# The fourth tile for U blocks ahead of the loop, kept in use for the last four blocks

## The chip, the cores and the metric

The kernel runs on one core of a Trainium2 chip. The metric is the time of one execution on the device in microseconds (us); the median of several executions counts. The engines are named as in the profile: PE (TensorE matmuls), DVE (VectorE), ACT (ScalarE), POOL (GpSimd) and SP (SyncE, which here only issues DMAs). ACT and POOL issue DMAs as well. Each engine takes its own instructions in their order; semaphores order them between engines.

## The reference

One encoder layer on 512 tokens of width 1024: LayerNorm, a joint projection, neighbourhood attention and latent attention, an output projection, LayerNorm, and then a feed-forward part with 16384 experts (PEER) and a gated embedding, followed by a last LayerNorm. The change sits in the feed-forward part, for a chunk of 128 tokens:

```
q = (xb @ w_q).reshape(128, 8, 256)
s1, s2 = q[..., :128] @ sub_keys[0].T, q[..., 128:] @ sub_keys[1].T
...top 16 of each, top 16 of their sums -> idx (128 tokens x 128 experts), g = softmax
u = u_table[idx]                       # 16384 x 1024
hpre = einsum('td,ted->te', xb, u)
act = g * gelu(hpre)
out = einsum('te,ted->td', act, v_table[idx])
```

## The kernel before

The 16384 experts are 128 blocks of 128. For most tokens the kernel does not gather rows: it multiplies every token with every expert and masks with a dense matrix G (tokens x experts, zero where an expert was not chosen).

**Which tokens go which way.** Chunk 0 (128 tokens) gathers its U and V rows by indirect DMAs of POOL, 128 of each (`gather_u`, L1349, and `gather_v`, L1358, into eight tiles `gat`; 26 of the U rows are done earlier, in `beside`, L1076); DVE multiplies each gathered tile. Chunk 1 gathers its U rows (`own_rows`). Chunks 2 and 3 (256 tokens) use dense U blocks: a block is 1024 x 128 numbers, 512 KB, and gives `ge = gelu(U block x tokens)`. For chunks 1 to 3 (384 tokens) V is dense.

**U blocks ahead of the loop.** Blocks 0 to 99 are computed before the main loop, by `lead_block` (L1134): eight float32 matmuls of 128x256 with `whole` (the 256 tokens), sixteen in the profile's records, 3.5 us a block. They fill PE while DVE routes and builds G. A block is loaded by `load_u` (L1102) through SP's DMA queue into one of four tiles: three tiles `raw` of the pool `wst`, taken in turn, and one tile `raw_u`, for every fourth block. A load waits until the last reader of its tile is done. Before the change the last four blocks (96 to 99) take `raw` tiles alone, so that `raw_u` has its last reader in block 95, and block 99 takes the tile of block 96. The matmuls of blocks 97 to 99 write PSUM tiles `hp`, those before them `mm`.

**What takes the place of raw_u.** After the blocks the pool of `raw_u` is closed (`pR.close()`, L1333), and tiles of the next pools are laid over it, among them one of the eight `gat` tiles: its first indirect DMA on POOL waits until the last matmul that reads `raw_u` is done.

**The main loop** (L1392) has 128 steps n. In each, DVE masks G (`dn`, L1426), ACT and DVE split the step's V block and its slice of G into two parts (`v_hi`, `v_lo`, `a_hi`, `a_lo`, L102 and L103), and PE adds 18 matmuls of 128x512 into `acc` (L1377). From n = 8 to n = 35 a step also has one of the U blocks 100 to 127 (`expert_in`, L789, 24 matmuls of 128x256, tiles `raw`, `whi`, `wlo`). Between these, DVE does gathers, one or two a step up to n = 8 and about three a step while U blocks last. V blocks come through SP (`v_raw`, three tiles, L1330), slices of G too (`gt`, four quarters, L1315); G was written to DRAM before, by twelve ACT-issued DMAs of 2 MB, four for each chunk (`g_dram<-g_st`, L1019, the last of them issued at 884.77 us).

**Order.** Up to the loop, all five queues keep the program's order (`manual_schedule`); in the loop only DVE and SP do. A load that is written earlier in the program stands earlier in SP's queue, and everything behind it waits with it. `h_s` and `gb` at L1086 are V blocks of the first two steps, loaded ahead.

Of the kernel before, what the change touches and what calls it, by code (L numbers as in the profile page):

```python
# [35 lines left out]
LEAD = 100  # L36
# [25 lines left out]
RAWS = 4  # L62
# [11 lines left out]
def tile_encoder_layer(ctx: ExitStack, tc: tile.TileContext, A: dict, out: bass.AP):  # L74
# [96 lines left out]
    def ps_tile(name, bufs=2):  # L171
        return ps6.tile([128, 512], F32, name=name, bufs=bufs)
# [924 lines left out]
    raws = []  # L1097
    tasks = []
    gating = True
    loaded = 0  # L1100

    def load_u():  # L1102
        nonlocal loaded
        if loaded < LEAD:
            if loaded % RAWS == RAWS - 1 and loaded < LEAD - 4:
                raw = rg.tile([128, 8, 128], F32, name="raw_u")
            else:
                raw = wst.tile([128, 8, 128], F32, name="raw", bufs=3)
            raws.append((loaded, raw))
            ins = nc.sync.dma_start(raw, A["uT"][loaded])  # L1110
            if not loaded:
                tc.keep_in_program_order(ins)
            loaded += 1
# [3 lines left out]
    def leave_u(i, ps):  # L1117
        k = i - SPILL
        if 0 <= k < KEPT:
            if k % 2 == 0:  # L1120
                name = ("g_raw", "g_raw", "g_hi", "g_lo")[k // 2]
                kept.append(pK.tile([128, 2, N_U], F32, name=name, bufs=2 if k < 4 else 1))
            ge = kept[k // 2][:, k % 2]
        else:
            ge = pB.tile([128, N_U], F32, name="ge", bufs=GES)
        nc.scalar.activation(ge, ps[:, :N_U], AF.Gelu)  # L1126
        if i < SPILL:
            nc.scalar.dma_start(ge_dram[i], ge)
        else:
            ge_t[i] = ge  # L1130
# [3 lines left out]
    def lead_block():  # L1134


        while len(raws) < (RAWS if loaded < LEAD - 4 else 3) and loaded < LEAD:
            load_u()
        if not raws:
            return  # L1140
        i, raw = raws.pop(0)
        ps = psH.tile([128, 512], F32, name="hp") if gating else ps_tile("mm", 4)
        for k in range(8):
            nc.tensor.matmul(ps[:, :N_U], raw[:, k], whole[:, k, :], start=(k == 0), stop=(k == 7))  # L1144
            if k == 3 and last:
                leave_u(*last.pop())
            if k % 2 and tasks:
                tasks.pop(0)()
            yield PRODUCT_U
        last.append((i, ps))  # L1150
# [52 lines left out]
    def gate_and_leads():  # L1203
        nonlocal gating
        graw = [gate_raw(0), gate_raw(1)]
        for n in range(FIRST):
            if n == FIRST - 2:
                w, cut = gate_cut(graw.pop(0))
                tasks.extend([cut[0], nothing, cut[1]])
            yield from lead_block()  # L1210
        for j in range(16):
            if j % 8 == 0:
                while tasks:
                    tasks.pop(0)()
                gps = [ps_tile("mm", 4) for _ in range(4)]
            k = j % 8
            for c in range(4):
                cs = slice(c * 128, (c + 1) * 128)
                mm3(gps[c], (hTh[:, k, cs], hTl[:, k, cs]), w, k == 0, k == 7)
                yield PRODUCT_G  # L1220
            if j + 1 < 16:
                w, cut = gate_cut(graw.pop(0))
                if j + 2 < 16:
                    graw.append(gate_raw(j + 2))
                tasks[0:0] = [cut[0], nothing, cut[1]]
            if k == 7:
                gate_end(gps, slice(j // 8 * 512, j // 8 * 512 + 512))
                yield from lead_block()
                yield from lead_block()
            yield from lead_block()  # L1230
# [34 lines left out]
    with tc.manual_schedule(engines={nc.vector.engine, nc.scalar.engine, nc.tensor.engine, nc.sync.engine,  # L1265
                                     nc.gpsimd.engine}):
        for _ in range(RAWS):
            load_u()
# [280 lines left out]
```

## Time and profile before

| | |
|---|---|
| median of 3 runs | 1527.5 us (1525.15 to 1528.54) |
| profiled execution, its own time | 1529.18 us |
| its span in the trace | 1527.2 us |
| PE busy | 1487.8 us (97%) |
| DVE busy | 1303.8 us (85%) |
| ACT, POOL busy | 658.2 us, 556.2 us |
| DMA, mean over the span | 301 GB/s |

Times in the rows are us from the start of the span. In a timeline row the columns are start, length, engine, line, operation, out<-in, shapes and count; in square brackets is the idle time of the engine before it, and what ended it. `SPq` is a DMA issue on SP's queue: its length is the issue, not the transfer. Blocks 0 to 99 lie between 410 and 910 us, the main loop from 909.5 us to 1510 us.

### The profile page before, as it was taken

The numbers are of one execution on the slowest core, as the hardware profiler recorded it, in microseconds if no ns is written. First come the engines' busy times: TensorE is split into PE (matmuls) and PEld (weight loads), VectorE is DVE, ScalarE is ACT, GpSimd is POOL, SyncE is SP. The second block draws the span as 40 slices with busy tenths as digits, with TensorE's granted clock in tenths as the row PEclk, the third lists the DMA queues.
The fourth block names the chain that finished last, engine by engine and source line by source line (L and its number), as shares of the span: only waits on it lengthen the run. The fifth ranks groups of instructions, "written<-read, shape, count | busy, mean of one in ns | idle before, by whom it ended". The sixth has DMA issues, their size and how long they took to land.

```text
span 1527.2 us, 23112 instructions
## 1 busy us (share of the span) xinstructions
PE 1487.8 (97%) x7747; PEld 1256.4 (82%) x7747; DVE 1303.8 (85%) x3020; ACT 658.2 (43%) x1226; POOL 556.2 (36%) x520
## 2 busy tenths in 40 slices
PE   8999899999999999999999989999999999999997
PEld 5788777788888889889888867888988888888885
DVE  6376686679989998888889947999999999999996
ACT  3355685333222666147515623343434333333342
POOL 1013110010015333353313424555555666666620
PEclk9999999999999999999999989999999999999999
DMA  6333240142379999999999988999999999999982
GB/s 229 102 111 97 84 125 29 42 142 83 104 228 334 346 408 383 413 398 415 406 379 353 410 353 304 415 411 414 415 411 411 410 412 410 410 412 411 412 321 77
DMA packets 194218, 459.38 MB, mean 301 GB/s; under 512 B 18226, under 2 KB 97970, under 8 KB 192564
## 3 DMA queue, kind: packets, MB, share of 16 engines
q1 hardware_dynamic: 121712, 214.08, 38.3%
q0 software_dynamic: 57984, 207.12, 34.6%
q10 hardware_dynamic: 14404, 36.71, 6.1%
q8 instruction: 61, 1.00, 0.3%
q14 instruction: 57, 0.47, 0.1%
HBM read 414.07 MB, written 40.89 MB: 298 GB/s over the span
## 4 chain that ended last, share of the span: by engine, by line
PE 79%; DVE 11%; DMA 6%; issue 2%; ACT 2%; POOL 0%; SPq 0%; DVEq 0%; ACTq 0%; POOLq 0%
PE acc L1377 33%; PE mm L1144 9%; PE hp L1144 4%; PE tr L1002 4%; PE mm L117 3%; PE mm L119 3%; PE mm L118 3%; PE pj L117 3%; PE pj L118 3%; PE pj L119 3%; DMA row<-in_u_rows_dram,s_ix 2%; PE hp L117 2%; PE hp L119 2%; PE hp L118 2%; DMA wlo<-in_u_rows_dram,s_ix 2%
## 5 line engine op out<-in xcount | busy, mean ns | idle before, releaser
L1360 POOL DMA_INDIRECT gat<-in_v_rows_dram,i_sel x128 | 211.4, 1652 | 120.2 <-DVE base L1362 99.2
L1144 PE MATMUL mm<-whole,raw 128*128 128x256 f32 x832 | 187.1, 379 | 0.9 <-DMA raw<-in_uT_dram 0.9
L102 ACT CAST whi<-raw 128x1024 fp32r<-128x1024 f32 (+4 forms) x117 | 117.3, 1003 | 149.8 <-PE mm L118 46.6
L1345 POOL DMA_INDIRECT gat<-in_u_rows_dram,i_sel x102 | 132.6, 1300 | 124.8 <-DVE hdot L1351 97.5
L1144 PEld LDWEIGHTS mm<-whole,raw 128*128 128x128 f32 x832 | 155.9, 190 | 21.2 <-ACT ge L1126 1.3
L1362 DVE SCALAR_TENSOR_TENSOR base<-gat,hdot,base 128x1024 f32<-128x1024 f32 x128 | 163.9, 1280 | 1.6
L103 DVE TENSOR_TENSOR wlo<-raw,whi 128x1024 fp32r<-128x1024 f32 (+4 forms) x117 | 135.5, 1159 | 33.2 <-ACT whi L102 32.9
L1377 PE MATMUL acc<-v_hi,a_hi 128*128 128x512 f32 x480 | 149.0, 391 | 2.4 <-ACT a_hi L102 2.2
L1377 PE MATMUL acc<-v_lo,a_hi 128*128 128x512 f32 x480 | 148.7, 390 | 0.1
L1377 PE MATMUL acc<-v_hi,a_lo 128*128 128x512 f32 x480 | 148.4, 389 | 0.0
L102 ACT CAST a_hi<-gt 128x384 fp32r<-128x384 f32 x126 | 64.6, 512 | 183.0 <-PE acc L1377 111.1
L102 ACT CAST v_hi<-v_raw 128x1024 fp32r<-128x1024 f32 x80 | 84.0, 1050 | 109.6 <-issue 58.1
L1057 POOL DMA_INDIRECT whi<-in_u_rows_dram,s_ix x51 | 53.8, 1055 | 200.6 <-DVE cand L905 132.3
L1351 DVE CUSTOM_DVE_ANT_0 scr<-gat,h 128x1024 f32<-128x1024 f32 x102 | 124.7, 1222 | 2.3
L1040 DVE TENSOR_SCALAR oh_j<-iota,eT 128x128 f32<-128x128 f32 x384 | 117.3, 379 | 0.0
L1377 PEld LDWEIGHTS acc<-v_lo,a_hi 128*128 128x128 f32 x480 | 90.0, 188 | 19.8 <-DVE v_lo L103 0.8
L1377 PEld LDWEIGHTS acc<-v_hi,a_lo 128*128 128x128 f32 x480 | 89.9, 188 | 19.1 <-DVE a_lo L103 0.2
L103 DVE TENSOR_TENSOR v_lo<-v_raw,v_hi 128x1024 fp32r<-128x1024 f32 x80 | 97.4, 1218 | 9.1 <-ACT v_hi L102 9.1
L1377 PEld LDWEIGHTS acc<-v_hi,a_hi 128*128 128x128 f32 x480 | 88.1, 188 | 19.9 <-ACT a_hi L102 3.0
L1002 PEld LDWEIGHTS tr<-oh_i,oh_j 128*128 128x128 f32 x768 | 94.3, 191 | 9.2 <-ACT g_st L1014 2.3
L1002 PE MATMUL tr<-oh_i,oh_j 128*128 128x128 f32 x768 | 97.2, 277 | 3.7 <-DVE oh_j L1040 3.7
L103 DVE TENSOR_TENSOR a_lo<-gt,a_hi 128x384 fp32r<-128x384 f32 x126 | 69.7, 553 | 33.2 <-ACT a_hi L102 31.8
(392 smaller groups left out, 3504.7 us busy)
## 6 DMA issues: line engine op xcount, KB each, us to landing
raw<-in_uT_dram SPq DMA_DIRECT2D x104, 512.0 KB
v_raw<-in_v_rows_dram SPq DMA_DIRECT2D x82, 512.0 KB
g_dram<-g_st ACTq DMA_DIRECT2D x12, 2048.0 KB
gt<-g_dram SPq DMA_DIRECT2D x60, 384.0 KB
raw<-in_v_rows_dram SPq DMA_DIRECT2D x44, 512.0 KB
raw_u<-in_uT_dram SPq DMA_DIRECT2D x24, 512.0 KB
ge_dram<-ge ACTq DMA_DIRECT2D x88, 128.0 KB
ge<-ge_dram SPq DMA_DIRECT2D x88, 128.0 KB
```

The lines of the kernel that those rows point to most:

```text
L102: nc.scalar.copy(hi, src)
L103: nc.vector.tensor_tensor(lo, src, r32(hi), op=OP.subtract)
L117: nc.tensor.matmul(ps, a[0], b[0], start=start, stop=False)
L118: nc.tensor.matmul(ps, a[0], b[1], start=False, stop=False)
L119: nc.tensor.matmul(ps, a[1], b[0], start=False, stop=stop)
L1002: nc.tensor.matmul(ps[:, i * 128:(i + 1) * 128], oj[:, 4 * r + i, :], oi[:, 4 * r + i, :], start=True, stop=True)
L1144: nc.tensor.matmul(ps[:, :N_U], raw[:, k], whole[:, k, :], start=(k == 0), stop=(k == 7))
L1345: nc.gpsimd.indirect_dma_start(out=u[:], out_offset=None, in_=u_rows, in_offset=bass.IndirectOffsetOnAxis(ap=i_sel[:, c, k:k + 1], axis=0))
L1351: nc.vector.tensor_tensor_reduce(scr, u, h[c], op0=OP.mult, op1=OP.add, accum_out=hdot[:, c, k:k + 1], scale=1.0, scalar=0.0)
L1360: nc.gpsimd.indirect_dma_start(out=u[:], out_offset=None, in_=v_rows, in_offset=bass.IndirectOffsetOnAxis(ap=i_sel[:, c, k:k + 1], axis=0))
L1362: nc.vector.scalar_tensor_tensor(base[c], u, hdot[:, c, k:k + 1], base[c], op0=OP.mult, op1=OP.add)
L1377: nc.tensor.matmul(acc[c][hf], a[:, cs], b[:, hf * 512:(hf + 1) * 512], start=(n == 0 and i == 0), stop=(n == 127 and i == 2))
```

## The change

Two conditions go. In `load_u` every fourth block takes `raw_u`, the last one (block 99) too. In `lead_block` four blocks are held loaded or under way up to the end, not three from block 96 on.

```diff
     def load_u():
         nonlocal loaded
         if loaded < LEAD:
-            if loaded % RAWS == RAWS - 1 and loaded < LEAD - 4:
+            if loaded % RAWS == RAWS - 1:
                 raw = rg.tile([128, 8, 128], F32, name="raw_u")
             else:
                 raw = wst.tile([128, 8, 128], F32, name="raw", bufs=3)
...
     def lead_block():
-        while len(raws) < (RAWS if loaded < LEAD - 4 else 3) and loaded < LEAD:
+        while len(raws) < RAWS and loaded < LEAD:
             load_u()
```

SP's queue at the end of the blocks ahead, before the change. `raw_u_8023` is block 95, the four `raw` at L1110 are blocks 96, 97, 98 and 99, `h_s` is the V block of step 1, `v_raw` are those of steps 2, 3 and 4, `gt0` quarters of G for steps 8 to 15:

```order
L1110 DMA raw_u_8023<-in_uT_dram 128x1024
L1086 DMA h_s_8111<-in_v_rows_dram 128x1024
L1110 DMA raw_8114<-in_uT_dram 128x1024
L1110 DMA raw_8159<-in_uT_dram 128x1024
L1110 DMA raw_8202<-in_uT_dram 128x1024
L1330 DMA v_raw_8249<-in_v_rows_dram 128x1024
L1315 DMA gt0_8378<-g_dram_3022 128x3x256
L1330 DMA v_raw_8380<-in_v_rows_dram 128x1024
L1110 DMA raw_8253<-in_uT_dram 128x1024
L1315 DMA gt0_8378<-g_dram_3022 128x3x256
```

The same stretch of SP's queue after the change:

```order
L1110 DMA raw_u_8023<-in_uT_dram 128x1024
L1110 DMA raw_8067<-in_uT_dram 128x1024
L1086 DMA h_s_8113<-in_v_rows_dram 128x1024
L1110 DMA raw_8116<-in_uT_dram 128x1024
L1110 DMA raw_8161<-in_uT_dram 128x1024
L1330 DMA v_raw_8251<-in_v_rows_dram 128x1024
L1110 DMA raw_u_8204<-in_uT_dram 128x1024
L1315 DMA gt0_8378<-g_dram_3022 128x3x256
L1330 DMA v_raw_8380<-in_v_rows_dram 128x1024
L1315 DMA gt0_8378<-g_dram_3022 128x3x256
```

Block 96 has moved ahead of `h_s`, and block 99, now `raw_u_8204`, ahead of a quarter of G and the V block of step 3. The rest of the queue reads alike.

The end of the blocks ahead in PE's queue, before the change (`tr` is work on G, `mm` and `hp` are U blocks at eight matmuls each, `acc` is step 0 of the loop):

```order
L1144 MATMUL mm<-whole,raw_u 128x256 x5
L1002 MATMUL tr<-oh_i,oh_j 128x128 x8
L1144 MATMUL mm<-whole,raw_u 128x256 x3
L1144 MATMUL mm<-whole,raw 128x256 x8
L1144 MATMUL hp<-whole,raw 128x256 x24
L1377 MATMUL acc_8240<-whi,a_hi 128x512
```

And after the change:

```order
L1144 MATMUL mm<-whole,raw_u 128x256 x5
L1002 MATMUL tr<-oh_i,oh_j 128x128 x8
L1144 MATMUL mm<-whole,raw_u 128x256 x3
L1144 MATMUL mm<-whole,raw 128x256 x8
L1144 MATMUL hp<-whole,raw 128x256 x16
L1144 MATMUL hp<-whole,raw_u 128x256 x8
L1377 MATMUL acc_8242<-whi,a_hi 128x512
```

Nothing moves on PE; block 99 is read from another tile. POOL's queue is the same, row by row.

## Rows read from the trace of the kernel before

**Rows 1.** The page's 40 slices of the span (38.2 us each): mean busy share of the 16 DMA engines in tenths.
```profile
DMA  6333240142379999999999988999999999999982
```

**Rows 2.** The chain of work that ended last, 850 to 980 us: start, length, what. A DMA piece runs from the issue to the landing.
```profile
888.89 14.34 DMA raw<-in_uT_dram
...
929.32 8.90 DMA raw<-in_uT_dram
```

**Rows 3.** The timeline of PE around the end of the blocks ahead (blocks 95, then 97 and 98, then 99) and in the first steps of the loop (n = 0, n = 1, n = 7).
```profile
883.95 1.46 PE L1144 MATMUL mm<-whole,raw_u 128*128 128x256 f32 x6
...
888.70 7.07 PE L1144 MATMUL hp<-whole,raw 128*128 128x256 f32 x32
903.36 6.52 PE L1144 MATMUL hp<-whole,raw 128*128 128x256 f32 x16 [7.60 <-DMA raw<-in_uT_dram]
909.54 0.81 PE L1377 MATMUL acc<-whi,a_hi 128*128 128x512 f32 x2
...
913.85 0.62 PE L1377 MATMUL acc<-whi,a_hi 128*128 128x512 f32 x2
...
940.70 0.73 PE L1377 MATMUL acc<-v_hi,a_hi 128*128 128x512 f32 x2 [2.21 <-ACT a_hi L102]
```

**Rows 4.** Windows: the stretch; its length, then busy us (and count) of PE, PEld, DVE, ACT and POOL; granted PE clock, DMA share, GB/s.
```profile
904.00:908.00 4.00, 4.00 (x11) 3.19 (x10) 2.86 (x6) 0.00 (x0) 2.98 (x2) 0.50 0.71 210
...
766.00:774.00 8.00, 7.12 (x33) 5.97 (x32) 6.13 (x30) 0.94 (x3) 2.83 (x3) 1.00 1.00 415
```

**Rows 5.** The timeline of SP's queue, 860 to 930 us (rows of several issues are merged: the three of 869.72 are blocks 96 to 98).
```profile
861.24 0.38 SPq L1086 DMA_DIRECT2D h_s<-in_v_rows_dram  x1
869.72 9.02 SPq L1110 DMA_DIRECT2D raw<-in_uT_dram  x3
878.84 0.37 SPq L1330 DMA_DIRECT2D v_raw<-in_v_rows_dram  x1
...
884.65 0.44 SPq L1330 DMA_DIRECT2D v_raw<-in_v_rows_dram  x1
888.89 0.33 SPq L1110 DMA_DIRECT2D raw<-in_uT_dram  x1
...
918.70 10.54 SPq L1330 DMA_DIRECT2D v_raw<-in_v_rows_dram  x3
```

**Rows 6.** DMA in four answers: all packets of 885 to 936 us; all packets of 895 to 903.2 us; and of 889 to 895 us the queues of ACT (q10) and SP (q1): packets, MB, share of 16 engines.
```profile
DMA packets 4984, 15.48 MB, mean 304 GB/s; under 512 B 442, under 2 KB 1978, under 8 KB 4854
...
DMA packets 1201, 3.40 MB, mean 415 GB/s; under 512 B 126, under 2 KB 452, under 8 KB 1201
...
q10 hardware_dynamic: 120, 1.82, 70.7%
...
q1 hardware_dynamic: 135, 0.27, 11.5%
```

**Rows 7.** The timeline of POOL: the fourth gather of the loop's eight tiles, which lies over `raw_u`, and the eighth.
```profile
885.68 0.94 POOL L1345 DMA_INDIRECT gat<-in_u_rows_dram,i_sel  x1 [4.60 <-PE mm L1144]
...
891.06 0.94 POOL L1345 DMA_INDIRECT gat<-in_u_rows_dram,i_sel  x1 [0.30 <-issue]
```

**Rows 8.** The timeline of ACT: the cast of `h_s`, the casts of step 3's V block and step 1's G slice, and the cast of U block 100.
```profile
886.09 1.05 ACT L102 CAST whi<-h_s 128x1024 fp32r<-128x1024 f32 x1
...
900.69 1.04 ACT L102 CAST v_hi<-v_raw 128x1024 fp32r<-128x1024 f32 x1 [3.57 <-DMA v_raw<-in_v_rows_dram]
...
901.91 0.50 ACT L102 CAST a_hi<-gt 128x384 fp32r<-128x384 f32 x1
...
938.24 1.04 ACT L102 CAST whi<-raw 128x1024 fp32r<-128x1024 f32 x1 [6.37 <-DMA raw<-in_uT_dram]
```

**Rows 9.** The timeline of DVE in steps 1 to 5: `a_lo` of steps 1 and 2, the multiplication of the fourth gathered tile, `v_lo` of steps 4 and 5.
```profile
902.45 0.56 DVE L103 TENSOR_TENSOR a_lo<-gt,a_hi 128x384 fp32r<-128x384 f32 x1 [8.38 <-ACT a_hi L102]
...
914.19 0.56 DVE L103 TENSOR_TENSOR a_lo<-gt,a_hi 128x384 fp32r<-128x384 f32 x1 [7.30 <-ACT a_hi L102]
...
915.92 1.23 DVE L1351 CUSTOM_DVE_ANT_0 scr<-gat,h 128x1024 f32<-128x1024 f32 x1
...
923.30 1.23 DVE L103 TENSOR_TENSOR v_lo<-v_raw,v_hi 128x1024 fp32r<-128x1024 f32 x1 [2.72 <-ACT v_hi L102]
...
927.66 1.22 DVE L103 TENSOR_TENSOR v_lo<-v_raw,v_hi 128x1024 fp32r<-128x1024 f32 x1
```

**Rows 10.** Timelines of four engines, in three pairs of an issue and the instruction that waited for its landing: a U block while a 2 MB write of G runs (SP, PE), a gather at 766.91 us in the same stretch (POOL, DVE), and a gather at 870.20 us (POOL, DVE).
```profile
762.33 3.78 SPq L1110 DMA_DIRECT2D raw<-in_uT_dram  x2
...
773.54 7.14 PE L1144 MATMUL mm<-whole,raw 128*128 128x256 f32 x32 [0.88 <-DMA raw<-in_uT_dram]
...
766.91 0.94 POOL L1057 DMA_INDIRECT wlo<-in_u_rows_dram,s_ix  x1 [1.36 <-DVE cv L827]
...
775.30 1.23 DVE L1059 CUSTOM_DVE_ANT_0 wlo<-wlo,h_s 128x1024 f32<-128x1024 f32 x1 [2.86 <-DMA wlo<-in_u_rows_dram,s_ix]
...
870.20 0.94 POOL L1057 DMA_INDIRECT wlo<-in_u_rows_dram,i_sel  x1 [1.97 <-DVE oh_j L1040]
...
876.12 1.22 DVE L1059 CUSTOM_DVE_ANT_0 wlo<-wlo,h 128x1024 f32<-128x1024 f32 x1 [1.19 <-DMA wlo<-in_u_rows_dram,i_sel]
```

**Rows 11.** Groups of instructions in 960 to 1500 us (PE) and in 950 to 1130 us (DVE): line, engine, operation, count, busy us, mean ns of one, idle us before.
```profile
L1377 PE MATMUL acc<-v_hi,a_hi 128*128 128x512 f32 x420 | 129.7, 390 | 0.0
...
L1351 DVE CUSTOM_DVE_ANT_0 scr<-gat,h 128x1024 f32<-128x1024 f32 x81 | 99.0, 1222 | 1.9
```

## The prediction

> **What bounds the kernel now.** I read the waits of PE first, then the chain of waits around the longest of them, then the queues (SP, POOL) and engines (ACT, DVE) that stand beside it.
>
> In the main loop PE has no idle time at all: its costliest group shows 0.0 us of it in 960 to 1500 us [rows 11]. So what PE reaches early at the loop's first steps stays gained to the end, if the others come as early. They are close: DVE idles only 1.9 us before its main group in 180 us of the loop [rows 11], and the DMA engines are busy to the full [rows 1].
>
> The place of the change is the seam before the loop. PE does blocks 97 and 98 without a gap, 7.07 us for both, so 3.5 us a block, and then stands still for 7.60 us, until the load of block 99 lands [rows 3]. That load is issued at 888.89 us, when block 96 ends and frees its tile, and takes 14.34 us [rows 2, 5]. After the pause the granted clock is 0.50 [rows 4], and block 99 takes from 903.36 to 909.54 us, 6.18 instead of 3.5 us [rows 3]. The loop then runs into one more wait: at step 7 PE idles 2.21 us [rows 3], because ACT's cast for step 7 stands behind the cast of U block 100, whose load (issued 929.32 us, 8.90 us long) ACT waits for [rows 2, 8]. From there on the loop is fed closely and PE never waits.
>
> **The change, part by part.**
>
> Earlier issue of block 99. Its new tile is free when block 95 ends, 883.95 + 1.46 = 885.4 us [rows 3], 3.5 us earlier than now. Before it in SP's queue stands the V block of step 2, which went out at 878.84 us [rows 5], so the queue has reached it. PE wants it at 888.70 + 7.07 = 895.8 us: there are 10.4 us for the transfer. How long it takes is not shown, so from both sides: as long as now, 14.34 us, would be 899.7 us. By the bytes: at most the V block of step 2 (0.52 MB), two gathers (1.05 MB), the last 2 MB write of G (2.10 MB) and itself (0.52 MB) go before, 4.2 MB. At the 415 GB/s of a full stretch [rows 6] that is 10.1 us, and it lands at 895.5 us. The nearest single transfer, a U block loaded while such a write ran, took 11.2 us (762.33 to 773.54 us) and cost PE 0.88 us [rows 10]. I take the bytes' bound, since five gathers leave the queue (next part), and so no pause: -7.6 us, and with it the slow clock, 6.18 - 3.5 = -2.7 us, and 0.2 us of step 0, which takes 4.31 us where the six steps behind it take 4.1 us (913.85 us to the pause that ends at 940.70 us) [rows 3]. PE starts the loop 10.3 us earlier, at 899.2 us, and step 1 is 10.5 us earlier.
>
> Gathers held back. The fourth of the loop's first eight gathers waits for the last reader of `raw_u`, now block 95, and goes out at 885.68 us, the fifth to eighth follow up to 891.06 us [rows 7]. With the change it waits for block 99, to about 899.4 us, and the four behind it on POOL with it: 2.6 MB leave the stretch in which block 99 is loaded. DVE reads the fourth tile at 915.92 us; from `a_lo` of step 1 to there it works 13.5 - 7.3 = 6.2 us [rows 9], so after the change it wants it at about 907.2 us, 7.8 us after the issue. Gathers that something waited for took 5.8 us (870.20 to about 876.0) and 8.3 us (766.91 to about 775.2) [rows 10]. I take 0; the bounds are 0 and +0.5 us.
>
> Moved behind. The quarter of G and the V block of step 3 (884.65 us) now go out after block 99's load, 1.6 us later. That V block is what ACT waits for at 900.69 us, with step 1's cast behind it [rows 8]. Bytes again: 4.2 + 0.39 + 0.52 = 5.1 MB, 12.3 us from 885.4, so 897.7 us at the earliest bound, 3 us before now; at the latest I take the 900.69 us of now, since 1.3 MB of gathers and more that ran beside it are gone. I take half of it, 899.2 us, and step 1's `a_lo` at 901.0 instead of 902.45 us.
> Block 96 goes before `h_s`: block 96 waits for its tile to 869.72 us [rows 5], and `h_s` leaves behind it, 9 us later than its 861.24 us. It is cast at 886.09 us [rows 8], 16 us later, more than any transfer above; nothing. Blocks 97 and 98 get half a megabyte in front of them, 1.3 us at 415 GB/s; they have 14 us from the issue to use, against 11.2 us in the row above; nothing, at worst the rest of 14.34 us, +0.4 us.
>
> What is late next. From step 1's `a_lo` (902.45 us) to the end of `v_lo` of step 5 (928.8 us) DVE takes 26.4 us, of which 7.30 + 2.72 us is idle time that hangs on PE, so 16.4 us of work [rows 9]. From 901.0 us on this ends at 917.4 us, 11.4 us earlier. On that `v_lo` hangs the third V load of the row at 918.70 us, behind it the load of U block 100 [rows 5], behind that ACT's casts and PE's step 7. If this load takes 8.9 us again, step 7 starts at 929.3 instead of 940.7 us: 11.4 us earlier. PE itself could be there at 899.2 + 7 x 4.1 = 927.9 us, so a wait of about 1.4 us stays in place of 2.2. From step 7 all goes as before.
>
> The sum: 10.5 us at the start of the loop, 0.9 us more by step 7, -11.4 us in all. Against the profiled execution (1529.18 us, span 1527.2 and 2.0 around it) that is 1517.8; the median of the runs shown lies 1.7 us lower, so 1516.1 us.
>
> Bounds of this: with step 1 fed no earlier than now, -10.0. At the other end PE can gain no more than 10.5 + 2.2 = 12.7 us up to step 7, and the DMA engines moved 15.48 MB in the 51 us from 885 to 936 us [rows 6], 37.3 us at 415 GB/s, so no more than 13.7 us can go.
>
> **The rivals.**
>
> Block 99 still late. While the write of G runs (889 to 895 us) SP's queue gets 0.27 MB, ACT's 1.82 MB [rows 6]; if the load gets no further in that time than now, its 14.34 us stay, it lands at 899.7 us and 4.0 us of the pause are left. For it speaks that share; against it the gathers that are gone. The clock then decides: after 7.60 us of pause it was 0.50, after 0.88 us it was 1.00 [rows 4], and the row nearer to 4.0 is the short one: 10.5 - 4.0 = 6.5 us gained, 1521 us; with the slow clock 3.6 us, 1524 us.
> The Trainium skill ("TensorE: Matmul & The Clock Gate", section "Part 1: The HAM clock gate") says that PE falls to half clock after one idle window of about 3.4 us and needs as much busy time to come back. Both rows agree with it, and by that rule a pause of 4.0 us would keep the slow clock: the 1524 us.
> The skill ("DMA: Bandwidth & Descriptors", section "Queues, rings and completion order") also says that each DMA engine takes turns between the queues, a packet at a time. It speaks for this rival: an earlier place in SP's queue does not pass ACT's write. The share of 11.5% against 70.7% of the engines' time [rows 6] agrees that SP's turns are thin there.
>
> Given back at step 7. The five gathers now fall together with the V, G and gather transfers of the first steps, where the DMA engines had room, 13.7 of 51 us. With 11.4 us gained only 2.3 us of that room is left. If block 100's load takes 13 to 15 us instead of 8.9, the gain is 5 to 7.5 us: 1520 to 1522.5 us. For it: 14.34 us is what a load took in a full stretch. Against: the room was enough in total.
>
> Slower: the held gathers starve DVE. DVE and POOL work in order; a fourth tile that lands later than DVE reads it today (915.92 us), 16.5 us after its issue, makes DVE later than before at step 3, one for one, and PE with it, having no slack in the loop. At 20 us, +3.5 us: 1531 us. Against it: 5.8 and 8.3 us in full stretches. That it decides needs twice the longer of them.
>
> Nothing: the load goes out earlier and what PE wins at the seam waits again at step 7, with block 100 landing no earlier than now. For that the DVE chain above would have to keep its 10.0 us of idle time, which hangs on PE. 1527.5 us.
>
> **How the numbers follow.** The forecast with its bounds (10.0 to 12.7 us, widened to 9 for small waits not seen here) gets 0.56, a gain of 12.7 to 14 us 0.12, given back at step 7 0.14, block 99 still late 0.10, nothing 0.05, slower 0.03. A measurement of this kernel can tell about 0.2% (3.1 us) from no change. Faster by more: 0.56 + 0.12 + 0.14 + 0.09 = 0.91 (a tenth of the late-block rival counts as no change); within: 0.06; slower: 0.03. The range takes in the forecast, the larger gain and the whole of what may be given back, and a part of the first rival: 5 to 15 us gained with the scatter of a median, 1512.5 to 1522.5 us.
>
> **What will show it.** In the profile after: PE goes from block 98 to block 99 without a wait on `raw_u`, with a granted clock of 1.00 from 888 to 912 us; the first `acc` matmul at about 899 us; POOL's fourth gather released by PE at about 899.4 us; ACT's cast of step 3's V block between 897.7 and 900.7 us; no DVE wait on a gathered tile; step 7 near 929 us behind the cast of block 100, and no idle time of PE behind step 10. It would be wrong if PE still waits at block 99, if DVE waits for `gat`, or if step 7 comes at 933 us or later.

## The result and the profile after

The changed kernel takes 1520.5 us (median of 8 runs, 1518.4 to 1524.6), the kernel before 1528.0 us beside it (8 runs, 1524.5 to 1536.9): a ratio of 0.9949, 95% interval 0.9932 to 0.9965, or 7.8 us less (5.3 to 10.4). The profiled execution took 1520.17 us with a span of 1518.1 us, 9.0 us less than the one before. Forecast were 1516.1 us and 11.4 us of gain.

PE around the end of the blocks ahead and in the loop's steps 0, 1, 7, 8 and 9, from its timeline in the kernel after:

```profile
888.57 7.07 PE L1144 MATMUL hp<-whole,raw 128*128 128x256 f32 x32
896.09 3.69 PE L1144 MATMUL hp<-whole,raw_u 128*128 128x256 f32 x16 [0.45 <-DMA raw_u<-in_uT_dram]
899.43 0.81 PE L1377 MATMUL acc<-whi,a_hi 128*128 128x512 f32 x2
...
903.75 0.62 PE L1377 MATMUL acc<-whi,a_hi 128*128 128x512 f32 x2
...
930.28 0.73 PE L1377 MATMUL acc<-v_hi,a_hi 128*128 128x512 f32 x2 [1.90 <-ACT a_hi L102]
...
936.49 0.62 PE L1377 MATMUL acc<-v_hi,a_hi 128*128 128x512 f32 x2
...
943.55 0.73 PE L1377 MATMUL acc<-v_hi,a_hi 128*128 128x512 f32 x2
```

The last row is step 9. The same two steps, 8 and 9, in the kernel before:

```profile
945.32 0.62 PE L1377 MATMUL acc<-v_hi,a_hi 128*128 128x512 f32 x2
...
952.58 0.73 PE L1377 MATMUL acc<-v_hi,a_hi 128*128 128x512 f32 x2 [0.15 <-issue]
```

Against [rows 3]: the pause before block 99 is 0.45 instead of 7.60 us, the block takes 3.69 instead of 6.52 us, step 0 comes 10.11 us earlier, step 1 10.10 us, step 7 10.42 us. Then the gain shrinks: step 8 starts 8.83 us earlier than before, step 9 9.03 us; step 10 comes 9.04 us earlier (950.80 and 959.84 us), and from there to the end both need the same 567.3 us.

The two loads in the chain of waits of the kernel after (start, length, what), that of block 99 and that of block 100:

```profile
885.30 10.65 DMA raw_u<-in_uT_dram
...
919.22 8.58 DMA raw<-in_uT_dram
```

Against [rows 2]: block 99's load goes out 3.59 us earlier and takes 10.65 instead of 14.34 us. Block 100's takes 8.58 instead of 8.90 us.

The packets that moved while block 99's load was under way, first in the kernel after (885.3 to 895.95 us), then in the kernel before (888.89 to 903.23 us), there with the row of POOL's queue, which carries the gathers:

```profile
DMA packets 1067, 4.40 MB, mean 413 GB/s; under 512 B 102, under 2 KB 474, under 8 KB 938
```

```profile
DMA packets 1589, 6.00 MB, mean 419 GB/s; under 512 B 146, under 2 KB 568, under 8 KB 1476
...
q0 software_dynamic: 721, 2.62, 44.7%
```

Both stretches are full. The load came in sooner because less went with it: 2.62 MB of gathers are in the old stretch, 0.65 MB in the new one. From 889 to 895 us of the kernel after, ACT's queue (q10) and SP's (q1), as in [rows 6]:

```profile
q10 hardware_dynamic: 101, 1.41, 54.9%
q1 hardware_dynamic: 524, 1.02, 43.5%
```

POOL's fourth gather, held until block 99 is done (timeline of POOL, after):

```profile
900.05 1.20 POOL L1345 DMA_INDIRECT gat<-in_u_rows_dram,i_sel  x1 [19.87 <-PE hp L1144]
```

ACT's casts: V block of step 3, V block of step 4, U block 100, U block 101 (timeline of ACT, after):

```profile
898.11 1.04 ACT L102 CAST v_hi<-v_raw 128x1024 fp32r<-128x1024 f32 x1 [1.25 <-DMA v_raw<-in_v_rows_dram]
...
912.11 1.05 ACT L102 CAST v_hi<-v_raw 128x1024 fp32r<-128x1024 f32 x1 [3.95 <-PE acc L1377]
...
927.82 1.05 ACT L102 CAST whi<-raw 128x1024 fp32r<-128x1024 f32 x1 [6.05 <-DMA raw<-in_uT_dram]
...
932.81 1.05 ACT L102 CAST whi<-raw 128x1024 fp32r<-128x1024 f32 x1 [2.58 <-DMA raw<-in_uT_dram]
```

DVE: `a_lo` of step 1, the multiplication of the fourth gathered tile, `v_lo` of steps 4, 5, 7 and 8 (timeline of DVE, after):

```profile
899.87 0.56 DVE L103 TENSOR_TENSOR a_lo<-gt,a_hi 128x384 fp32r<-128x384 f32 x1 [5.94 <-ACT a_hi L102]
...
905.96 1.23 DVE L1351 CUSTOM_DVE_ANT_0 scr<-gat,h 128x1024 f32<-128x1024 f32 x1
...
913.19 1.23 DVE L103 TENSOR_TENSOR v_lo<-v_raw,v_hi 128x1024 fp32r<-128x1024 f32 x1 [2.57 <-ACT v_hi L102]
...
917.55 1.22 DVE L103 TENSOR_TENSOR v_lo<-v_raw,v_hi 128x1024 fp32r<-128x1024 f32 x1
...
929.85 1.23 DVE L103 TENSOR_TENSOR v_lo<-v_raw,v_hi 128x1024 fp32r<-128x1024 f32 x1 [4.01 <-ACT v_hi L102]
...
934.83 1.23 DVE L103 TENSOR_TENSOR v_lo<-v_raw,v_hi 128x1024 fp32r<-128x1024 f32 x1 [1.81 <-ACT v_hi L102]
```

The kernel before has the cast of block 101 (ACT) and `v_lo` of step 8 (DVE) as follows:

```profile
941.84 1.05 ACT L102 CAST whi<-raw 128x1024 fp32r<-128x1024 f32 x1 [1.20 <-DMA raw<-in_uT_dram]
```

```profile
943.87 1.23 DVE L103 TENSOR_TENSOR v_lo<-v_raw,v_hi 128x1024 fp32r<-128x1024 f32 x1 [0.43 <-ACT v_hi L102]
```

Two things are to be seen here. The 7.30 us of DVE's idle time in [rows 9] are gone, the 2.72 us in front of step 4's `v_lo` are not (2.57 us): its cast waits until PE is done with the buffer. And block 101 is now late: its cast waits 2.58 us where the kernel before shows 1.20 us, and DVE stands 1.81 us before step 8's `v_lo`, before 0.43 us.

Windows over step 7, where PE starts again after its pause (columns as in [rows 4]); first the kernel after, then the kernel before:

```profile
930.00:932.00 2.00, 1.60 (x4) 0.99 (x5) 2.00 (x3) 0.23 (x1) 0.00 (x0) 0.83 0.95 387
932.00:934.00 2.00, 2.00 (x6) 1.59 (x5) 1.02 (x3) 1.19 (x2) 0.95 (x1) 0.50 0.99 344
934.00:936.00 2.00, 2.00 (x8) 1.58 (x8) 1.17 (x2) 1.21 (x2) 0.00 (x0) 0.82 1.01 370
```

```profile
940.00:942.00 2.00, 1.19 (x4) 0.59 (x4) 1.73 (x3) 0.80 (x3) 0.00 (x0) 1.00 0.99 404
942.00:944.00 2.00, 2.00 (x11) 1.65 (x10) 1.57 (x4) 2.00 (x3) 0.63 (x1) 1.00 0.82 238
```

After a pause of 1.90 us the granted clock fell to 0.50 and step 7 took 6.21 us; in the kernel before it stayed at 1.00 after 2.21 us, and step 7 took 4.62 us.

### The profile page after: what moved, and what is told of

Read it like the earlier page. It is cut to its first block, busy times and chain, and to the rows that moved or that the text cites. A ratio compares the mean times of both kernels' runs of the same rounds, so it can differ in the third digit from the quotient of the medians.

```text
span 1518.1 us, 23113 instructions
## 1 busy us (share of the span) xinstructions
PE 1486.6 (98%) x7747; PEld 1255.5 (83%) x7747; DVE 1304.0 (86%) x3020; ACT 659.0 (43%) x1226; POOL 556.0 (37%) x520
## 4 chain that ended last, share of the span: by engine, by line
PE 73%; DVE 11%; DMA 9%; issue 3%; ACT 2%; POOL 1%; SPq 0%; DVEq 0%; POOLq 0%; ACTq 0%
PE acc L1377 33%; PE hp L1144 4%; DMA whi<-in_u_rows_dram,s_ix 4%; PE mm L117 3%; PE mm L1144 3%; PE mm L119 3%; PE pj L117 3%; PE mm L118 3%; PE tr L1002 3%; PE pj L118 3%; PE pj L119 3%; PE hp L117 2%; PE hp L119 2%; PE hp L118 2%; DMA wlo<-in_u_rows_dram,s_ix 2%
```

## The experiments

Executions differ by some 7 us before they reach the place of the change (last section), so each trace is read from the end of block 95's last matmul with `raw_u` (885.41 us before, 885.27 us after). The table has, from there, the starts of steps 0, 7 and 10 in us; the pause of PE before block 99 and the longest later pause, with its step; and the distance from step 7 to step 9, which is 11.03 us where nothing waits (runs 6, 8 and 11). From step 10 to the end all need 567.2 to 567.5 us, but for run 7, which needs 569.0 and pauses twice more on PE (0.36 and 0.70 us, at 1026 and 1169 us). Line numbers of the experiments are up to 9 higher than in the kernel before.

| run | median, us | ratio to before, 95% interval | before block 99 | step 0 | longest later pause | step 7 | 7 to 9 | step 10 |
|---|---|---|---|---|---|---|---|---|
| before | 1527.0 to 1528.1 | 1 | 7.60 | 24.13 | 2.21 (7) | 55.29 | 11.88 | 74.43 |
| after | 1520.5 | 0.9949 [0.9932, 0.9965] | 0.45 | 14.16 | 1.90 (7) | 45.01 | 13.27 | 65.53 |
| 1 after, again | 1521.7 | 0.9946 [0.9925, 0.9968] | 0 | 13.68 | 1.89 (7) | 44.49 | 13.29 | 65.04 |
| 2 second edit alone | 1529.3 | 1.0002 [0.9987, 1.0018] | 7.63 | 22.81 | 2.27 (7) | 54.04 | 13.16 | 74.18 |
| 3 before, gathers held | 1523.8 | 0.9970 [0.9954, 0.9985] | 2.33 | 16.46 | 1.70 (7) | 47.12 | 11.73 | 66.10 |
| 4 after, not held | 1522.8 | 0.9958 [0.9943, 0.9972] | 0.53 | 14.24 | 3.07 (7) | 47.72 | 12.38 | 67.31 |
| 5 after, not held, other order | 1522.0 | 0.9955 [0.9932, 0.9977] | 0.79 | 14.49 | 2.68 (7) | 46.97 | 12.54 | 66.73 |
| 6 U loads early | 1523.2 | 0.9953 [0.9934, 0.9973] | 0.30 | 14.01 | 4.95 (5) | 50.59 | 11.03 | 68.61 |
| 7 block 101 early | 1519.5 | 0.9944 [0.9919, 0.9970] | 0.57 | 14.27 | 2.32 (7) | 45.53 | 13.12 | 65.62 |
| 8 U loads earlier | 1517.5 | 0.9923 [0.9894, 0.9952] | 0 | 13.76 | none | 42.53 | 11.03 | 60.54 |
| 9 after, a third time | 1521.8 | 0.9961 [0.9944, 0.9978] | 0.44 | 14.14 | 1.91 (7) | 44.99 | 13.26 | 65.47 |
| 10 as 8, again | 1514.9 | 0.9919 [0.9906, 0.9932] | 0.92 | 14.62 | 0.19 (7) | 43.87 | 11.56 | 62.55 |
| 11 as 8, on before | 1524.8 | 0.9980 [0.9969, 0.9992] | 7.70 | 23.31 | none | 52.10 | 11.03 | 70.12 |
| 12 block 100 earlier | 1517.8 | 0.9929 [0.9915, 0.9944] | 0.35 | 14.05 | 1.45 (8) | 42.85 | 13.97 | 64.04 |

### Run 1: the changed kernel as the yardstick

> The changed kernel once more, as the yardstick of the three runs beside it. Both theories expect what it did: some 7.8 us below the kernel before (5.3 to 10.4), no PE wait of more than 0.5 us at block 99 and the loop's first step at about 899.4 us of the span.

It did what it did before: no pause at block 99 at all this time, step 7 to step 9 again 13.3 us. Its times in the span are 1.1 to 1.2 us higher because block 95 ended 1.66 us later, less the pause that it did not have.

### Run 2: the second edit alone

```diff
-        while len(raws) < (RAWS if loaded < LEAD - 4 else 3) and loaded < LEAD:
+        while len(raws) < RAWS and loaded < LEAD:
```

> Only the second edit: four loads are held ahead at the end as well, but block 99's goes into one of the three shared tiles. Its load then stands ahead of G's quarter and the V block of step 3 in SP's queue and waits there for block 96's last matmul, at about 888.9 us, and the fourth gather is released by block 95 as before. If the earlier issue is what gains (my theory), nothing is gained at block 99: it lands at 899 to 903 us, PE waits 4 to 8 us, and the V block of step 3, now queued behind it, leaves 4 us later than before; the time is that of the kernel before, -2 to +3 us. If the place ahead of the other loads is enough (the rival), the pause is under 1 us and the gain 7 us or more.

Nothing gained. The chain of waits, PE's timeline, and SP's issues of step 3's V block and of block 99:

```profile
887.38 14.38 DMA raw<-in_uT_dram
```

```profile
901.89 5.17 PE L1144 MATMUL hp<-whole,raw 128*128 128x256 f32 x16 [7.63 <-DMA raw<-in_uT_dram]
```

```profile
883.10 0.48 SPq L1330 DMA_DIRECT2D v_raw<-in_v_rows_dram  x1
887.38 0.33 SPq L1110 DMA_DIRECT2D raw<-in_uT_dram  x1
```

The load still waits for block 96's tile, goes out 3.5 us after block 95's end, takes as long as in [rows 2], and PE stands as long. One expectation missed: the load is written earlier in the program, but it did not move in SP's queue. It went out behind the quarter of G and behind step 3's V block, as in [rows 5], so the rule given above, that a load written earlier stands earlier in the queue, does not hold for this load, whose tile was not free. The place in the program is worth nothing without a free tile; what a place ahead of those two loads alone would be worth was not tested. (The first edit alone was not tried: block 99 would then be loaded into a tile of a pool that is already closed.)

### Run 3: the gathers held, and nothing else

```diff
+        if i == LEAD - 1:
+            nc.tensor.matmul(ps[:, N_U:2 * N_U], u_tile[0][:, 0], whole[:, 0, :], start=True, stop=True)
```

The matmul reads block 95's tile (`u_tile[0]`).

> The kernel before, with one more small matmul at the end of block 99 that reads the fourth tile into a part of PSUM that nothing reads. So the fourth to eighth gathers are held to block 99's end as in the changed kernel, while block 99's load keeps its tile and its issue at 888.9 us. If the gathers that are gone from the stretch are what makes the load quick (the rival), it takes some 8 us in place of 14.34, lands at about 897 us, PE's pause is 1 to 2 us with no slow clock behind it, and most of the gain is there: 6 to 8 us. If it is the 3.5 us earlier issue that gains and the gathers do not count, the load takes 14.3 us again and the time is that of the kernel before, within 2 us. Between, 3 to 5 us, both have a share.

In the trace step 10 comes 8.3 us earlier, of the changed kernel's 8.9; by the ratios it gains 4.6 us (2.3 to 7.0) where run 1 beside it gains 8.2. The chain of waits, the timeline of PE, then that of POOL:

```profile
885.59 11.98 DMA v_raw<-in_v_rows_dram
897.59 1.05 ACT v_hi L102
898.64 0.29 ACT ge L1126
```

```profile
899.04 3.69 PE L1145 MATMUL hp<-whole,raw 128*128 128x256 f32 x16 [2.33 <-ACT ge L1126]
```

```profile
903.44 1.18 POOL L1350 DMA_INDIRECT gat<-in_u_rows_dram,i_sel  x1 [21.30 <-PE hp L1154]
```

The load goes out at 889.84 us, and PE starts block 99 at 899.04 us, no longer behind the load: block 99 waits for its PSUM tile, whose evacuation (`ge`) stands on ACT behind the cast of step 3's V block. So the load took at most 9.2 us, with the five gathers out of its way. The forecast counted the gathers' absence only as a help to the earlier issue; alone it is worth a little over half of the whole change by the ratios, and nearly all of it in the one trace.

### Runs 4 and 5: the earlier issue, gathers not held

```diff
-        u = pG.tile([128, D], F32, name="gat", bufs=GATS)
+        u = gat()    # tiles gat0 to gat7, named, in the order 0 1 2 3 4 6 7 5
```

Run 5 takes them in the order 0 1 2 4 6 7 3 5.

> The changed kernel, with the eight gather tiles taken in another order, so that the one that lies over the fourth tile comes last: the fourth to seventh gathers are not held to block 99's end, only the eighth is. Block 99's load is issued at 885.4 us as in the changed kernel. If the held gathers are what made room, 2.1 MB are back in the stretch, 5 us at 415 GB/s: the load takes 13 to 15 us instead of 10.65, PE waits 2.5 to 4.5 us at block 99, and the kernel is 2.5 to 7 us slower than the changed one (the larger number with the slow clock). If they do not count, the time is that of the changed kernel within 1 us; the gathers being out of the loop's first steps, the load of U block 101 may even land 1 us earlier.

> The changed kernel with the eight gather tiles in a third order: as in the run before, only the eighth gather waits for block 99, and the tile that lay over h_s, and held the fourth gather there to 890.5 us, now comes seventh. So the fourth to sixth gathers may go out before or beside block 99's load and not behind it. If a load's place among the bytes in flight decides how long it takes (my theory), up to 1.6 MB more stand ahead of it, 3.8 us at 415 GB/s: 12 to 14.5 us from its issue to its landing, a PE wait of 2 to 4 us at block 99, and 3 to 6 us more than the changed kernel. If the earlier issue alone is enough (the rival), the load takes 10 to 11 us again and PE waits under 1 us. The V block of step 3 should take about 16 us again in both cases.

In both the fourth gather went out behind block 99's load (890.51 us against 886.73; 886.66 against 884.39), released by DVE, so the test of gathers that stand ahead of it was not made. Block 99 was in time (0.53 and 0.79 us of pause). What came late was the transfer behind it. Run 4's chain of waits and PE's timeline:

```profile
888.08 16.48 DMA v_raw<-in_v_rows_dram
```

```profile
906.36 0.72 PE L1386 MATMUL acc<-whi,a_hi 128*128 128x512 f32 x2 [0.98 <-ACT a_hi L103]
```

The V block of step 3 took 16.48 us, its cast held up step 1's, and PE waited 0.98 us at step 1 and 3.07 us at step 7. Run 5's took 16.05 us. Counted to step 10, not holding the gathers costs 1.8 us (run 4) and 1.2 us (run 5); the ratios of runs 4, 5 and 1 lie within each other's intervals. From its issue to its cast the V block takes 11.5 us (after) and 12.0 us (run 3) where the gathers are held, and 16.0 us (before) and 16.1 to 16.5 us (runs 4 and 5) where they are not, whether block 99's load goes out early or late. The theory, up to here: two loads must land by about 898 us, block 99's and step 3's V block; either the earlier issue or the held gathers bring the first, and only the held gathers bring the second.

### Runs 6, 8 and 10: blocks 100 to 102 loaded early

```diff
+EARLY = {5: 100, 6: 101, 7: 102}
...
             if n not in v_cut:
                 raw = v_next.pop(n, None) or load_v(n)
+            if n in EARLY:
+                u_early[EARLY[n]] = wst.tile([128, 8, 128], F32, name="raw", bufs=3)
+                nc.sync.dma_start(u_early[EARLY[n]], A["uT"][EARLY[n]])
```

The block's casts (`expert_in`) then read that tile instead of loading one. Runs 8 and 10 have steps 4, 5 and 6 in place of 5, 6 and 7.

> The changed kernel with U blocks 100, 101 and 102 loaded three steps earlier, behind the V loads of steps 5, 6 and 7 in SP's queue (from about 904 us), into the tiles that are free then. If the loads of blocks 100 and 101 are what costs PE its 1.90 us before step 7 and DVE its 4.01 and 1.81 us (my theory), both waits go: step 7 starts at 928.2 us, step 9 at 939 to 940, step 10 at 946.3 to 947.5 instead of 950.80, and the kernel is 3 to 4.5 us faster than the changed one, 11 to 13 us below the kernel before. If DVE's own work or the gathers are late anyway (the rival), a wait on a gathered tile or on DVE takes their place, and step 10 stays at 949.5 to 951: under 1.3 us gained.

> As the run with blocks 100 to 102 loaded early, one step earlier still: behind the V loads of steps 4, 5 and 6 (from about 896.7 us, where the DMA engines had room in the changed kernel, 217 to 257 GB/s). If room decides, blocks 100 to 102 land still earlier and step 10 starts at 946.3 to 947 us, 4 to 4.5 us before the changed kernel's. If what is put ahead there makes the held gathers late (the rival), DVE waits for a gathered tile at step 2 or 3, 1 to 3 us, and the run is no better than the one with the later place.

> The version with U blocks 100 to 102 loaded behind the V loads of steps 4 to 6 once more. If what its first trace showed holds (no PE wait from block 97 to the end, step 10 60.5 us behind the end of block 95, 5.0 us before the changed kernel's), it is 4 to 6 us faster than the changed kernel beside it. If the first run was luck of one execution, under 2 us.

Run 6 missed: step 10 comes 3.1 us later than in the changed kernel, and its ratio, 0.9953, is no better than run 1's 0.9946, each within the other's interval. The rival named there was wrong too: no gathered tile was late. SP's issue and ACT's cast of block 101, and what PE saw:

```profile
911.19 0.46 SPq L1410 DMA_DIRECT2D raw<-in_uT_dram  x1
```

```profile
925.85 1.04 ACT L103 CAST whi<-raw 128x1024 fp32r<-128x1024 f32 x1 [6.42 <-DMA raw<-in_uT_dram]
```

```profile
927.36 1.22 PE L1384 MATMUL acc<-v_hi,a_hi 128*128 128x512 f32 x2 [4.95 <-ACT a_hi L103]
```

The load took some 14.5 us, in the stretch where the held gathers and the V blocks fill the DMA engines, and ACT's order, which is not written out in the loop, had put its cast ahead of step 5's `a_hi`: a load issued earlier was also wanted earlier. One step earlier, in run 8, it found room: block 100's load had landed when its cast came up, and block 101's cast waited only 0.50 us for its data (timelines of SP and ACT, run 8):

```profile
897.75 0.38 SPq L1410 DMA_DIRECT2D raw<-in_uT_dram  x1
...
905.84 0.38 SPq L1410 DMA_DIRECT2D raw<-in_uT_dram  x1
```

```profile
904.92 1.05 ACT L103 CAST whi<-raw 128x1024 fp32r<-128x1024 f32 x1 [3.76 <-PE acc L1384]
...
914.59 1.05 ACT L103 CAST whi<-raw 128x1024 fp32r<-128x1024 f32 x1 [0.50 <-DMA raw<-in_uT_dram]
```

In run 8 PE has no pause any more from block 97 to the end, and step 10 comes 13.9 us before that of the kernel before. Run 10 confirms it beside run 9: a ratio of 0.9919 [0.9906, 0.9932] against 0.9961 [0.9944, 0.9978]; in its trace PE pauses 0.92 us before block 99, and step 10 comes 2.9 us before run 9's, where run 8 came 5.0 us before the changed kernel. It is the fastest version here, 12.4 us below the kernel before (10.4 to 14.4).

### Run 7: block 101 alone, early

```diff
+EARLY = {6: 101}
```

> As the run before, but block 101 alone is loaded early, behind the V load of step 6 (about 909 us); block 100 as in the changed kernel. If it is block 101's late landing that gives back 1.4 us between steps 7 and 9 (my theory), step 7 stays at about 930.3 us, up to 1.3 us later for the 0.5 MB put ahead of block 100, DVE's 1.81 us before the V cast of step 8 goes, and step 9 starts 13.0 us or less behind step 7, against 13.27 in the changed kernel and 11.88 in the kernel before: 11.5 to 12.2. If the slow clock of step 7 is what costs (the rival), step 9 stays 13.2 us behind step 7 wherever the clock falls again.

The theory fell. Block 101's cast found its data (no wait at 928.75 us), DVE did not idle before step 8, and step 9 had its operands 1.2 us early; yet step 9 came 13.12 us behind step 7, hardly less than 13.27. The clock in this run's windows:

```profile
930.00:932.00 2.00, 2.00 (x5) 1.58 (x6) 2.00 (x5) 1.02 (x2) 0.43 (x1) 0.50 0.77 262
```

So the slow clock alone costs it. Run 2 agrees: clock 0.50, operands 1.2 us early at step 9, 13.16 us.

### Run 9: the changed kernel a third time

> The changed kernel a third time, to stand beside the next two runs on the same chip: 6 to 9 us below the kernel before, PE's wait of about 1.9 us at step 7, step 10 about 65.0 to 65.5 us behind the end of block 95's last matmul.

PE's wait and step 10 came as expected; the gain, 6.0 us by the ratio (3.4 to 8.6), lies at the lower end of the 6 to 9 us. The trace's span is 1523.5 us, since block 95 ends at 890.71 us.

### Run 11: the early loads in the kernel before

> The same three early loads in the kernel before. Block 99's late landing, 7.6 us of pause and the slow clock behind it stay, since nothing of that is touched (step 0 again about 24 us behind the end of block 95); what the early loads can remove is the 2.2 us wait at step 7 and the DVE waits of steps 9 and 10: step 10 at 70.9 instead of 74.4 us behind block 95, 3.5 us gained. If the three loads (1.6 MB) crowd the full stretch before 908 us instead, a V block or block 99 is later and nothing is gained or up to 3 us are lost. With the run before it this tells whether the two changes add up: 3.5 us here and 4.5 to 5 there.

The block-99 pause stayed (7.70 us), the later pauses went, and step 10 came 4.3 us earlier. With the 8.9 us of the change that makes 13.2, and runs 8 and 10 have 13.9 and 11.9: the two add up in the traces. By the ratios runs 11 and 9 make 3.1 + 6.0 = 9.1 us, run 10 has 12.4; with intervals of about 2 us each that is no contradiction.

### Run 12: block 100 alone, earlier

```diff
+EARLY = {4: 100}
```

> As the version with three early loads, but block 100's alone, behind the V load of step 4; blocks 101 and 102 as in the changed kernel. PE's wait at step 7 should go, and with it the slow clock; block 101's load is then the next late one, issued when the V load of step 7 or 8 has gone, and lands at about 930 to 933 us: a wait of 0 to 3 us comes up at step 8 in place of the one at step 7. Step 10: if only the slow clock cost something behind step 7, 60.5 to 61.5 us behind the end of block 95, as with all three early; if block 101's landing costs as much by itself, 62 to 64.5 us; the changed kernel has 65.5.

The pause at step 7 went, and one of 1.45 us came up at step 8, behind block 101, with no slow clock (1.00 throughout). Step 10 lies at 64.04: block 101's landing costs by itself, 3.5 us more than run 8. With runs 7, 4 and 5 it shows what lies behind step 7: the late block alone gives 12.4 to 12.5 us from step 7 to step 9 (runs 4 and 5, clock 1.00; 14.0 in run 12, where step 7 itself comes 2.2 us earlier), the slow clock alone 13.1 (runs 2 and 7), both 13.3 (the changed kernel), neither 11.0. They lie beside each other, so that taking away one brings little. In the changed kernel's own steps the loss shows at step 7, 6.21 us instead of 4.62; step 8 took 7.06 instead of 7.26.

## Why the prediction was right, and where it was not

The place, the mechanism and the size of the first part held:

- Block 99's load. Forecast: out at 885.4 us, landed by 895.5 by the bytes' bound, no pause. Measured: 885.30 us, landed at 895.95, pause 0.45 us (0 to 0.57 us in runs 1, 9 and 7). The bytes' bound held because it counted what went with the load: 4.2 MB forecast, 4.40 MB moved. Runs 2 and 3 correct the reason: the prediction put the gain on the earlier issue, with the gathers' absence as what makes room. The earlier issue alone was enough for block 99 (runs 4 and 5, where the gathers went out behind it), and the absence alone nearly so (run 3, pause 2.33 us, and that behind a cast).
- The rival "block 99 still late" fell: with the write of G under way the load took 10.65 us, not 14.34. The thin share of SP's queue [rows 6] was no fixed one: from 889 to 895 us it has 43.5% now, 11.5% before. In run 3, with the gathers held and nothing else, it has 27.8% from 890 to 896 us, and ACT's queue 70.2%, as before, so what the gathers had went to SP. The turns between the queues that the Trainium skill ("DMA: Bandwidth & Descriptors", section "Queues, rings and completion order") tells of were the ground for this rival; no run here shows the turns themselves, nor why SP's share was so thin before.
- The slow clock behind that pause, 2.7 us, is gone: block 99 took 3.69 us.
- The held gathers: forecast issue 899.4 us, measured 900.05; no DVE wait on a gathered tile. DVE read the fourth tile at 905.96 us, 1.2 us before the forecast time of 907.2 us and 5.9 us after the issue, hardly more than the 5.8 us of [rows 10]: the cost was nothing, with little to spare.
- Step 3's V block: forecast 899.2 us, halfway between bounds; measured 898.11 us. Runs 4 and 5 show that this is what the held gathers pay for: counted from block 95's end, the cast starts at 12.8 us with them held, and at 17.9 and 17.5 us without.

Two terms failed, 2.4 us together, which is the difference of 11.4 to 9.0 us:

- "What is late next" took all 10.0 us of DVE's idle time out and counted 16.4 us of work. Both pieces hang on PE: ACT's casts wait there for buffers that PE frees, so DVE can come no earlier than PE lets it, and PE came 10.1 us earlier. At step 2 the 7.30 us went, since step 1's `a_lo` had moved by only 2.58 us and PE by more than both together. At step 4 the cast again waits for PE: 2.57 of the 2.72 us stayed, and `v_lo` came 10.11 us earlier (923.30 to 913.19 us), just as PE did. The prediction's 11.4 us were more than the 10.5 us that it gave PE itself. Step 5's `v_lo` ended at 918.77, not 917.4 us; block 100's load, 0.3 us shorter, gave a little back, and step 7 came 10.4, not 11.4 us earlier.
- "From step 7 all goes as before" lost 1.4 us: 13.27 us from step 7 to step 9 instead of 11.88. A wait of about 1.4 us at step 7 was forecast, 1.90 came, and the slow clock behind it was not in the sum at all, since [rows 4] and the 2.21 us pause of [rows 3] showed a clock of 1.00 after short pauses. Block 101's load, 923.07 to 932.8 us, came late in the now full stretch beside it; by runs 7 and 12 either of the two alone leaves most of the loss (step 10 5.1 and 3.5 us behind run 8's, where the changed kernel is 5.0 us behind). The rival "given back at step 7" had the right stretch and reason, and the wrong load and size: block 100's took 8.58 us, not 13 to 15. A load of 14.5 us there does occur, in run 6.

The gain by the ratio (7.8 us, 5.3 to 10.4; 8.2 and 6.0 us by the ratios of runs 1 and 9) is a little under the trace's 9.0 us, and run 3's is well under its trace's. One trace stands for one execution; where the others lose more is left open. That 7.8 us lie below the forecast's own band of 9 to 12.7 us and just above the 5 to 7.5 us of the rival "given back at step 7": the mechanism at block 99 was right, but the number is held only by a range wide enough to take in that rival.

## What to carry to other kernels

Before counting a transfer as late by its issue time, list what is already in flight in front of it and what is wanted next behind it: here taking away five gathers that nobody needed yet brought the load in nearly as well as issuing it earlier, and only that saved the transfer behind it. When idle time of an engine is to be taken out of a chain, ask of each piece which engine it hangs on: the chain can come no earlier there than that engine does, here 10.1 us and not 11.4. And an early load helps only if it finds room and if the order of its consumer does not move with it: one step made the difference between 3.1 us lost (run 6) and 5.0 and 2.9 us gained (runs 8 and 10) in the traces.

## What the runs showed of the hardware

Between 1.9 and 3.1 us, the granted clock after a pause of PE in this stretch does not follow the pause's length. It fell to 0.50 after 1.89, 1.90 and 1.91 us (three executions of the changed kernel), 2.27 (run 2) and 2.32 us (run 7); it stayed at 1.00 after 1.45 (run 12), 1.70 and 2.33 (run 3, at step 7 and before block 99), 2.21 (before), 2.68 (run 5) and 3.07 us (run 4). After the longer ones, 4.95 us (run 6) and 7.60 to 7.70 us (before, runs 2 and 11), it had fallen each time. In the blocks ahead the same wait, before the same work, came out both ways: after 1.97 us (run 9, at 725 us) the clock was 0.50, after 1.99 us (run 12, at 724 us) it was 1.00. Run 4 after its pause of 3.07 us:

```profile
934.00:936.00 2.00, 1.47 (x5) 0.86 (x6) 2.00 (x3) 0.37 (x1) 0.00 (x0) 1.00 0.83 340
```

In the changed kernel, where it fell, step 7 took 6.2 us instead of the 4.6 us of the kernel before. The Trainium skill ("TensorE: Matmul & The Clock Gate", section "Part 1: The HAM clock gate") lets the clock fall after an idle window of about 3.4 us; the measurement differs below that, 1.9 us were enough, and agrees above it. It also says that the window runs free of the kernel. That would let one pause fall into one window and another across two; no run here shows the windows, so it stays open.

The blocks ahead scatter by 7 us between executions of what is the same code there: block 95 ended between 883.4 and 890.7 us. The two latest, runs 9 and 12, had longer waits for DVE's one-hot tiles (7.0 and 6.1 us in all, 3.7 us in the kernel before) and for one U block (1.9 us instead of 0.9), and behind some of them the clock fell too. Run 9, PE's timeline and its window:

```profile
753.51 2.05 PE L1002 MATMUL tr<-oh_i,oh_j 128*128 128x128 f32 x8 [3.48 <-DVE oh_j L1040]
```

```profile
750.00:760.00 10.00, 6.53 (x30) 5.91 (x30) 7.67 (x20) 3.67 (x10) 2.84 (x3) 0.83 1.00 370
```

In the kernel before the longest such wait from 690 to 800 us is 1.08 us. A change of 1.4 us can't be read from medians under such scatter; counted from block 95's end, the three executions of the changed kernel agree within 0.5 us.
